# A decoder step's mixing stage: u projections by feature block, and the state-space part ranked ahead of banded attention

## The chip, the cores and the metric

The kernel runs on one core of a Trainium2 chip. A core has five engines with instruction queues of their own, each worked off strictly in order: TensorE (PE in the profile; PEld is its weight load) for matrix products, VectorE (DVE), ScalarE (ACT), GpSimd (POOL) and SyncE (SP, which here only issues DMAs). The metric is the time of one execution on the device in microseconds; several runs of each kernel are compared by their medians.

## The reference

One step of a one-layer hybrid decoder for 1024 prompt tokens and 32 sample tokens (8 sequences of 4), 1056 in all, 1024 features wide, in 32-bit floats:

```python
h = h + 0.5 * rms_norm(swiglu(rms_norm(h, ffn1_pre_g), ...), ffn1_post_g)
z = rms_norm(h, mix_pre_g) @ w_in                # 512 u, 512 q, 128 k, 128 v
y, s_re, s_im = s5_scan(u, s0_re, s0_im, ...)    # 32 groups of 16 features, 64 complex states each
g = gelu(y)
y_ssm = g * sigmoid(g @ ssm_w_glu + ssm_b_glu)
o = swa_prompt(q, k, v, sinks)                   # window 128, 8 heads on 2 key heads, sinks
mixed = concatenate([rms_norm(y_ssm), rms_norm(o)]) @ w_out
h = h + rms_norm(mixed, mix_post_g)
h = h + rms_norm(memory_attend(...), xa_post_g)  # 4 heads into 256 memory tokens
h = h + 0.5 * rms_norm(swiglu(rms_norm(h, ffn2_pre_g), ...), ffn2_post_g)
```

The sample tokens go through the same layer with a cached window and a state of their own. The memory keys and values of the prompt are projected in the same launch and are outputs too.

## The kernel before

Activations lie transposed, features on the 128 partitions and tokens along the free axis, in three token groups of 352, which are taken in the order 2, 0, 1 (`ORDER`). A large product is computed three times with operands split into a rounded high part and a remainder (`mm3`, line 105): high by high, high by low, low by high. Each weight is loaded by SP, split by ScalarE (line 99) and VectorE (line 100).

The program runs: first feed-forward, then the **mixing stage**, then the output projection w_out, cross-attention and the second feed-forward. In the mixing stage stand, in the order of the text:

1. the q, k and v projections, with the rotary part (`rope`, lines 807 to 831);
2. attention over 128-query blocks, of which 5, 6 and 7 come first. Each block is worked in two *halves* of four heads. A half has its scores (line 877, two products of 128 x 512 into PSUM tiles called ac), their masked maximum on VectorE (line 880), exponentials on ScalarE (line 850), sums and reciprocal (848 to 854), scaling on VectorE (856), eight transposes on TensorE (893), two copies out (897, one on VectorE, one on ScalarE), the value products into the tile po (900), and two copies into qT (903). `attend` issues the scores of the next half ahead of the combination of the present one; there are two score buffers, which lie in the block K3, and two ac tiles;
3. the u projections: four blocks of 128 features by three token groups, twelve products of 24 matmuls each into two PSUM tiles px, with an eviction that scales by the norm (line 922). Their inputs are the split activations X of the three token groups;
4. the state-space part `ssm()`: for each of four feature blocks a `gather` (transposes, lines 947 to 965, through PSUM tiles su and buffers ut, us, ug of the pool s1), then for pairs of groups `advance` (978 to 988: two products into sab, a rotation, a scan along the blocks, a rotation back) and `emit` (1000 to 1015), then `spread` (1022, 1028, 1031), and the gelu;
5. the memory projections `memory_kv` (lines 105 and 495, into px, with evictions 485 and 499): 384 matmuls of 256 columns that depend on nothing in this stage;
6. the sample tokens' attention, then blocks 0 to 2, a norm (`arm`, lines 151, 125 to 133, 143), blocks 3 and 4, a norm;
7. the gated linear unit, GLU (1162 to 1180), whose split inputs go into K2, K3 and a new X.

Pool s1 is allocated on the left side once pool x1, which holds the X of this stage, has been released; a tile of s1 waits for the readers of the tiles that lay in its place. The keys of attention (kz) lie in K2, the u of the four blocks in K0 and K1.

The order on each engine isn't that of the text. A scheduler gives each instruction the running number `tc.cur_priority` as its rank, walks through a model of the engines in time, and lets each engine take the lowest rank that is ready. The call `at(base + P)` sets the running number, so the constants `P_...` rank the parts of this stage against each other: attention 0, state space 10000, u 20000, GLU 25000, memory projections 30000. Attention of step 6 goes on where step 2 left off (`at(mark)`), right behind it.

Of the kernel before, what the change touches and what calls it, by code (L numbers as in the profile page):

```python
# [17 lines left out]
NH = 22  # L18
EPS = 1e-6
ORDER = (2, 0, 1)  # L20
P_ATT, P_SSM, P_U, P_GLU, P_MEM = 0, 10000, 20000, 25000, 30000
MAGIC = 12582912.0
PASSES = ((0, 0), (0, 1), (1, 0))
G_FFN1_PRE, G_FFN1_POST, G_MIX_PRE, G_MIX_POST, G_XA_PRE, G_XA_POST, G_FFN2_PRE, G_FFN2_POST, G_MEM, G_CAT = range(10)
# [3 lines left out]
def decoder_step(tc, a, o):  # L28
# [42 lines left out]
    def pbank():  # L71
        return pbase.tile([128, 512], F32, name="px", tag="px", bufs=2)
# [22 lines left out]
    def loadw(src, raw=None, width=1024):  # L95
        if raw is None:
            raw = stage(src, width=width)
        w = wp.tile([128, 2, 1024], F32R, name="w", tag="w", bufs=6)[:, :, :width]
        sc.activation(w[:, 0], raw, AF.Copy)  # L99
        v.tensor_sub(w[:, 1], raw, w[:, 0].bitcast(F32))  # L100
        return w
# [651 lines left out]
    for i in range(2):  # L753
        c = slice(512 * i, 512 * i + 512)
# [38 lines left out]
    def proj(w, t, p=None):  # L793
        p = bank() if p is None else p
        for k in range(8):
            mm3(p[:, :NT], w, k * 128, mid[t], k, k == 0, k == 7)
        return p[:, :NT]
# [119 lines left out]

    at(base + P_U)
    wu = [loadw(a["w_in"][c]) for c in range(4)]
    for t in ORDER:  # L920
        for c in range(4):
            v.tensor_mul(uT[c // 2][:, c % 2, t * NT:(t + 1) * NT], proj(wu[c], t, pbank()), mid[t][2])
    xp[0].release()
    sp_ = xp[0] = pool("s1", "left")
# [602 lines left out]
```

## Time and profile before

| | |
|---|---|
| median of 3 runs | 2352.02 us (2351.97 to 2355.77) |
| the profiled execution | 2350.7 us, span 2348.9 us |
| first feed-forward, to the q, k, v projections | up to about 815 us of the span |
| q, k, v projections | about 815 to 895 |
| u projections | 895 to 946 |
| state space, attention, memory projections | 946 to 1152 |
| GLU, then w_out | 1152 to 1181, from 1181 |

A row of a timeline has the start in us, the length in us, the engine, the line, the operation, output and inputs by the program's names without their numbers, the shape, and how many instructions were merged; in brackets the idle time ahead of it and what ended it. A row of a group has the count, the busy time in us, the mean length of one in ns, and idle time before with its releaser. A 32-bit matmul of plain operands leaves two records; one on split operands, or a transpose, leaves one. Records on an engine overlap, so a group's lengths add up to more than the time it takes. The granted clock is TensorE's, as a share of full speed.

### The profile page before, as it was taken

How to read it: one execution, taken by the hardware profiler on the slowest of the kernel's cores; microseconds unless marked ns; L12 is line 12 of the kernel's file. 1: busy time of each engine (PE TensorE's matmuls, PEld its weight loads, DVE VectorE, ACT ScalarE, POOL GpSimd, SP SyncE). 2: the span in 40 equal slices, each digit the busy share in tenths (PEclk: the TensorE clock that was granted, in tenths of full speed). 3: DMA queues.
4: the chain of work that ended last, by engine and by line, in shares of the span. 5: the costliest groups of instructions: out<-in, count | busy, mean ns of one | idle time of the engine just before them, and what ended most of it. 6: DMA issues, size and time to landing. Idle time of an engine off the chain costs nothing.

```text
span 2348.9 us, 37434 instructions
## 1 busy us (share of the span) xinstructions
PE 2281.9 (97%) x14425; PEld 2178.3 (93%) x14425; DVE 1631.5 (69%) x4004; ACT 839.4 (36%) x1645; POOL 15.9 (1%) x54
## 2 busy tenths in 40 slices
PE   8999999999999899999799989999999899999997
PEld 8999999999999899888699869999999899999996
DVE  8756556665664877777768855588866987776464
ACT  6322111211212433535545323354433434344443
POOL 0000000000000000000000000000000000000000
PEclk9999999999999999999899999999999999999998
DMA  4222212221213321544135562165544243326663
GB/s 171 70 71 68 62 57 71 82 76 59 73 55 93 112 87 58 193 147 127 35 97 167 183 221 72 55 213 169 175 132 144 85 143 106 115 97 200 185 193 119
DMA packets 112194, 272.39 MB, mean 116 GB/s; under 512 B 13168, under 2 KB 54128, under 8 KB 110576
## 3 DMA queue, kind: packets, MB, share of 16 engines
q1 hardware_dynamic: 78976, 227.81, 30.8%
q10 hardware_dynamic: 33040, 42.20, 5.1%
q8 instruction: 113, 1.85, 0.3%
q14 instruction: 65, 0.53, 0.1%
HBM read 229.87 MB, written 43.20 MB: 116 GB/s over the span
## 4 chain that ended last, share of the span: by engine, by line
PE 85%; DVE 7%; DMA 5%; ACT 2%; issue 1%; ACTq 0%; SPq 0%; DVEq 0%
PE mm L105 39%; PE mm L241 14%; PE mm L330 13%; PE mm L385 3%; PE px L105 3%; DMA raw<-wd 2%; DVE w L100 1%; PE cv L1279 1%; PE cs L1254 1%; PE px L1176 1%; DVE K L219 1%; PE ac L877 1%; PE px L495 1%; PE px L385 1%; DMA K<-h 1%
## 5 line engine op out<-in xcount | busy, mean ns | idle before, releaser
L105 PE MATMUL mm<-X,w 128*128 128x352 f32 x6384 | 1060.8, 325 | 12.3 <-ACT X L195 6.5
L105 PEld LDWEIGHTS mm<-X,w 128*128 128x128 f32 x6384 | 1028.3, 189 | 30.2 <-ACT X L195 8.5
L99 ACT ACTIVATE w<-raw 128x1024 fp32r<-128x1024 f32 (+1 forms) x271 | 266.2, 988 | 500.4 <-PE mm L105 212.2
L100 DVE TENSOR_TENSOR w<-raw,w 128x1024 fp32r<-128x1024 f32 (+1 forms) x271 | 307.1, 1136 | 136.2 <-ACT w L99 134.0
L241 PE MATMUL mm<-hid,w 128*128 128x352 f32 x2112 | 358.6, 328 | 12.6 <-DVE K L247 6.2
L241 PEld LDWEIGHTS mm<-hid,w 128*128 128x128 f32 x2112 | 345.6, 189 | 19.7 <-DVE K L247 8.8
L330 PE MATMUL mm<-xq,w 128*128 128x352 f32 x1584 | 263.5, 323 | 0.0
L330 PEld LDWEIGHTS mm<-xq,w 128*128 128x128 f32 x1584 | 255.9, 188 | 0.4 <-ACT w L310 0.4
L247 DVE TENSOR_TENSOR K<-K,mm 128x352 f32<-128x352 f32 x320 | 158.3, 518 | 52.2 <-PE mm L241 51.3
L514 DVE TENSOR_TENSOR K<-K 128x128 f32<-128x128 f32 (+7 forms) x796 | 171.6, 250 | 11.3 <-DMA sp<-K 2.0
L385 PE MATMUL mm<-xq,w 128*128 128x352 f32 x924 | 159.1, 326 | 4.6 <-ACT w L99 3.4
L385 PEld LDWEIGHTS mm<-xq,w 128*128 128x128 f32 x924 | 148.8, 188 | 10.7 <-ACT w L99 5.9
L310 ACT ACTIVATE w<-raw 128x512 fp32r<-128x512 f32 x154 | 90.0, 625 | 119.1 <-PE mm L330 83.1
L231 DVE TENSOR_TENSOR q<-mm,rs 128x352 f32<-128x352 f32 x88 | 46.0, 522 | 117.6 <-PE mm L105 117.6
L311 DVE TENSOR_TENSOR w<-raw,w 128x512 fp32r<-128x512 f32 x154 | 101.1, 686 | 6.2 <-ACT w L310 3.9
L116 DVE TENSOR_TENSOR tot<-tot,sq 128x352 f32<-128x352 f32 x179 | 93.0, 520 | 10.4 <-ACT sq L114 7.0
L114 ACT ACTIVATE sq<-K 128x352 f32<-128x352 f32 x170 | 81.9, 490 | 42.7 <-DVE tot L116 34.7
L229 DVE TENSOR_TENSOR sg<-mm,rs 128x352 f32<-128x352 f32 x88 | 46.0, 523 | 72.9 <-PE mm L105 72.5
L183 ACT ACTIVATE hid<-sg 128x352 fp32r<-128x352 f32 x88 | 43.6, 496 | 145.7 <-DVE sg L232 115.7
L230 ACT ACTIVATE sg<-sg 128x352 f32<-128x352 f32 x88 | 43.2, 492 | 138.9 <-DVE sg L229 120.4
L195 ACT ACTIVATE X<-K,c_gains 128x352 fp32r<-128x352 f32 x80 | 44.0, 580 | 45.4 <-DVE K L220 42.8
L184 DVE TENSOR_TENSOR hid<-sg,hid 128x352 fp32r<-128x352 f32 x88 | 45.8, 521 | 15.6 <-ACT hid L183 15.4
(326 smaller groups left out, 2179.1 us busy)
## 6 DMA issues: line engine op xcount, KB each, us to landing
raw<-wd SPq DMA_DIRECT2D x66, 512.0 KB
raw<-wu SPq DMA_DIRECT2D x65, 512.0 KB
raw<-wg SPq DMA_DIRECT2D x64, 512.0 KB
sp<-sp SPq DMA_DIRECT2D x16, 848.0 KB
h<-K ACTq DMA_DIRECT2D x9, 1408.0 KB
raw<-hs SPq DMA_DIRECT2D x66, 176.0 KB
raw<-wd SPq DMA_DIRECT2D x44, 256.0 KB
K<-xT SPq DMA_DIRECT2D x24, 352.0 KB
```

What stands on the lines that cost most here:

```text
L99: sc.activation(w[:, 0], raw, AF.Copy)
L100: v.tensor_sub(w[:, 1], raw, w[:, 0].bitcast(F32))
L105: pe.matmul(p, w[:, wa, col:col + 128], x[xa][:, k, :n], start=first and i == 0, stop=last and i == 2)
L114: sc.activation(q, c, AF.Square)
L116: eng.tensor_add(tot, tot, q)
L241: pe.matmul(p[c][:, :NT], w[j][:, wa, c * 128:c * 128 + 128], h[:, j, xa], start=j == 0 and i == 0, stop=j == 1 and i == 2)
L247: v.tensor_add(acc[:, c], acc[:, c], p[c][:, :NT])
L310: sc.activation(w[:, 0], x, AF.Copy)
L311: v.tensor_sub(w[:, 1], x, w[:, 0].bitcast(F32))
L330: pe.matmul(p, w[a_][:, wa, k * 128:k * 128 + 128], x[b_][xa][:, k], start=start and k == 0 and i == 0, stop=stop and k == 3 and i == 2, s ...
L385: pe.matmul(p[c][:, :NT], w[:, wa, c * 128:c * 128 + 128], (hi, lo)[xa], start=k == 0 and q == 0, stop=k == NH - 1 and q == 2)
L514: v.tensor_tensor(out, x, y, op)
```

## The change

Two edits. The ranks become u 0, state space 5000, attention 10000; GLU and memory projections keep theirs. And the twelve u projections are written with the feature block in the outer loop and the token group in the inner, where it was the other way round. No instruction is added or taken away.

```diff
-P_ATT, P_SSM, P_U, P_GLU, P_MEM = 0, 10000, 20000, 25000, 30000
+P_U, P_SSM, P_ATT, P_GLU, P_MEM = 0, 5000, 10000, 25000, 30000
...
     at(base + P_U)
     wu = [loadw(a["w_in"][c]) for c in range(4)]
-    for t in ORDER:
-        for c in range(4):
+    for c in range(4):
+        for t in ORDER:
             v.tensor_mul(uT[c // 2][:, c % 2, t * NT:(t + 1) * NT], proj(wu[c], t, pbank()), mid[t][2])
     xp[0].release()
     sp_ = xp[0] = pool("s1", "left")
```

## The prediction

> **What bounds the kernel now.** I read the page first, then the busy times by stage, then TensorE and VectorE in the stage that the change touches.
>
> ```profile
> span 2348.9 us, 37434 instructions
> PE 2281.9 (97%) x14425; PEld 2178.3 (93%) x14425; DVE 1631.5 (69%) x4004; ACT 839.4 (36%) x1645; POOL 15.9 (1%) x54
> ```
>
> TensorE is busy for 97% of the span. A mere reordering adds and removes no instruction, so it can win only TensorE's idle time or lose by adding some. The stages around the change (columns: stretch, length, busy time of each engine with its records, clock, DMA share, GB/s):
>
> ```profile
> 895.00:946.17 51.17, 51.17 (x312) 49.10 (x311) 48.04 (x130) 19.53 (x51) 0.00 (x0) 1.00 0.26 83
> 946.17:1117.42 171.25, 170.98 (x1343) 139.47 (x1342) 132.29 (x500) 80.90 (x223) 3.60 (x12) 1.00 0.46 154
> 1117.42:1151.46 34.04, 25.41 (x140) 16.70 (x138) 28.87 (x85) 22.82 (x61) 0.00 (x0) 0.88 0.20 59
> 1151.46:1181.44 29.98, 26.81 (x151) 26.81 (x151) 18.08 (x58) 15.19 (x30) 0.00 (x0) 0.80 0.04 8
> ```
>
> The first row is the u projections, the second the state-space part, attention and the memory projections together: TensorE is full in both. The third is the **tail of attention**: the memory projections, the only work that can fill every gap, are used up, and TensorE is idle for 8.6 us of 34.0 while VectorE is at 85%. The fourth is the gated unit (GLU). The tail's two ends, on TensorE, and VectorE's last steps in it:
>
> ```profile
> 1116.50 1.07 PE L495 MATMUL px<-w 128*128 128x256 f32 x7
> 1117.42 1.02 PE L877 MATMUL ac<-K,qT 128*128 128x512 f32 x2
> 1118.27 0.60 PE L893 MATMUL ac<-c_ident,K 128*128 128x128 f32 x4
> 1149.49 1.97 PE L900 MATMUL po<-K,vT 128*64 128x256 f32 x8 [2.04 <-DVE K L897]
> 1154.63 3.89 PE L1176 MATMUL px<-K,w 128*128 128x352 f32 x12 [3.17 <-ACT sq L1179]
> 1122.23 0.48 DVE L499 TENSOR_SCALAR mo<-px,rc 128x256 f32<-128x256 f32 x1
> 1145.31 1.14 DVE L856 TENSOR_SCALAR K<-K,ta 128x256 f32<-128x256 f32 x4
> 1148.65 0.68 DVE L897 COPY K<-ac 128x512 f32<-128x512 f32 x1
> ```
>
> From the last half block's value product (1149.49) the order of work is the same in both programs, so the question is when that product ends (1151.46 now).
>
> **The change part by part.** *u projections by feature block.* The twelve products stay, 288 matmuls. With the three token groups of block 0 done first, the state-space gather could begin after three of twelve products. The order on TensorE (px: a projection, su: a gather's transposes), before and now:
>
> ```order
> L105 MATMUL px_9606<-X1_8393,w_9359 128x352
> L947 MATMUL su_9697<-c_ident_94,K0_8467 128x128 x4
> ...
> L105 MATMUL px_9658<-X1_8393,w_9369 128x352
> L151 MATMUL px_10632<-ones_96,tot_10588 128x1
> ...
> L947 MATMUL su_9703<-c_ident_94,K0_8467 128x128 x4
> ```
>
> ```order
> L105 MATMUL px_9476<-X0_8082,w_9359 128x352
> L947 MATMUL su_9697<-c_ident_94,K0_8467 128x128 x4
> ...
> L105 MATMUL px_9658<-X1_8393,w_9369 128x352
> L877 MATMUL ac_9118<-K2_8466,qT_8465 128x512
> L151 MATMUL px_10632<-ones_96,tot_10588 128x1 x2
> L947 MATMUL su_9703<-c_ident_94,K0_8467 128x128 x4
> ```
>
> The first four transposes move up by seven products, but the second four still come behind the last one: their predecessor's copy goes into pool s1, which lies where the projections' inputs X lay, and all X are now in use to the end. The first state-space matmul (L978) moves up by 8 of TensorE's instructions. TensorE is full here, so I take 0 for this part; a late eviction would cost at most one product, 51.17 / 12 = 4.3 us, and a gain is excluded by 51.17 busy of 51.17.
>
> *State space before attention.* This pushes attention's halves back, past the memory projections. The end of those (L495) on TensorE, before and now (po: a half's value product, sy: a state-space emission):
>
> ```order
> L495 MATMUL px_11114<-w_11146,w_10586 128x256
> L877 MATMUL ac_11623<-K2_8466,qT_8465 128x512
> L893 MATMUL ac_11644<-c_ident_94,K3_9053 128x128 x4
> L1000 MATMUL sy_10533<-ug_10289,sp_10494 128x8
> ...
> L900 MATMUL po_11643<-K1_8468,vT_8460 64x256 x2
> ```
>
> ```order
> L495 MATMUL px_11114<-w_11146,w_10586 128x256
> L900 MATMUL po_11434<-K1_8468,vT_8460 64x256 x2
> L877 MATMUL ac_11454<-K2_8466,qT_8465 128x512
> L1000 MATMUL sy_10515<-ug_10289,sp_10455 128x8
> ...
> L900 MATMUL po_11434<-K3_9053,vT_8460 64x256 x2
> L877 MATMUL ac_11458<-K2_8466,qT_8465 128x512
> ```
>
> po_11643 is half 0 of block 3, with three halves behind it: four halves in the tail. po_11434 is half 0 of block 1: eight halves (one nearly done), and two emissions in place of one. So much leaves the full stage and goes behind it, by TensorE's groups in 946.17 to 1117.42:
>
> ```profile
> L877 PE MATMUL ac<-K,qT 128*128 128x512 f32 (+1 forms) x47 | 24.0, 590 | 0.2 <-DVE ta L880 0.2
> L893 PE MATMUL ac<-c_ident,K 128*128 128x128 f32 x88 | 14.4, 278 | 0.0
> L900 PE MATMUL po<-K,vT 128*64 128x256 f32 x88 | 13.7, 401 | 0.0
> 1105.47 0.28 PE L1000 MATMUL sy<-ug,sp 128*128 128x8 f32 x2
> 1108.01 1.67 PE L495 MATMUL px<-w 128*128 128x256 f32 x12
> 1112.58 0.93 PE L143 MATMUL ac<-c_ident,ti 118*128 118x118 f32 x6
> ```
>
> Seven score matmuls (two records each) at 24.0/47 = 0.51 a record: 7.1 us. 24 transposes at 0.164: 3.9. 16 value matmuls (32 records) at 0.156: 5.0. One emission, 1105.47 to 1108.01: 2.5. One reduction pair for a norm: 0.93 and about as much, 1.8. Together 20.3; but records overlap. The score at 1117.42 lasts 1.02 and the transposes behind it start after 0.85, at 1118.27, a factor of 0.83, which gives 16.9. I take **17 us**: the memory projections end at 1117.4 - 17 = 1100.4. The bounds are 20.3 (no overlap) and 171.25/1343 x 106 records = 13.5.
>
> *The longer tail.* VectorE's groups in the old tail, and one reduction with its successor's start:
>
> ```profile
> L184 DVE TENSOR_TENSOR X<-q,X 128x352 fp32r<-128x352 f32 x8 | 3.7, 517 | 0.0
> L100 DVE TENSOR_TENSOR w<-raw,w 128x1024 fp32r<-128x1024 f32 x3 | 3.7, 1221 | 0.0
> L856 DVE TENSOR_SCALAR K<-K,ta 128x256 f32<-128x256 f32 x12 | 3.4, 347 | 0.0
> L897 DVE COPY K<-ac 128x512 f32<-128x512 f32 x4 | 2.7, 682 | 0.0
> L1153 DVE SCALAR_TENSOR_TENSOR q<-qT,c_gains,rs 128x352 f32<-128x352 f32 x5 | 2.7, 572 | 0.0
> L1031 DVE SCALAR_TENSOR_TENSOR K<-K,c_gains,su 128x512 f32<-128x512 f32 x2 | 2.3, 1142 | 0.0
> L1168 DVE TENSOR_TENSOR X<-K,X 128x352 fp32r<-128x352 f32 x4 | 1.8, 516 | 0.0
> 1123.60 0.48 DVE L880 CUSTOM_DVE_ANT_0 K<-ac,c_mask,c_sinks 128x256 f32<-128x256 f32 x1 [0.74 <-PE ac L877]
> 1124.01 0.08 DVE L880 DVE_READ_ACCUMULATOR2_ANT ta<- 128x1 f32 x1
> ```
>
> A row overlaps the next by some 0.075 us (0.48 long, successor after 0.41), so each costs its mean less that, and the accumulator's read nothing. From the eviction of the last memory product (L499) to the copy of the last half (L897) VectorE now has 24 reductions (9.8), 4 weight splits L100 (4.6), 24 scalings (6.4), 7 copies (4.2), 2 L1031 (2.1), 12 L184 (5.3), 4 L1167 and 4 L1168 (2.8), 5 L1153 (2.5), 3 L116 (1.3) and small ones (4.7): **43.7 us**. By the same count the old program has 23.2, and took 1122.23 to 1148.65, 26.4.
>
> The waits in the new tail, walked along the two orders: 4.4 at its head, where TensorE has two emissions, four scores, eight transposes and three value pairs (5.1 + 3.8 + 1.2 + 1.9 = 12.0) before VectorE, with 8.7 of its own, can reduce the fourth score, and a weight split (1.1) stands ahead of that; 1.7 where the halves of blocks 0 to 2 drain and the norm of token group 0 runs before block 3's first reduction; 5.8 over the last four halves. With the 2.8 from the last copy to the end of its product (1148.65 to 1151.46) the tail is 43.7 + 11.9 + 2.8 = 58.4, near **58**. It replaces 34.0: **58 - 34 - 17 = +7 us**. The bounds: with no waits 46.5, so -4.5 (-8 with 20.3 for 17); at the old tail's 34.04/4 = 8.5 a half for 7.5 halves 64, so +13 (+16.5 with 13.5).
>
> What works the other way is within the sum. The preparation of the GLU's operands, which now stands between the last half's scaling and copy, has moved ahead. VectorE's last rows, before and now:
>
> ```order
> L856 TENSOR_SCALAR K3_9053<-K3_9053,ta_11716 128x256 x4
> L184 TENSOR_TENSOR X2_11913<-q_11926,X2_11912 128x352
> ...
> L1153 SCALAR_TENSOR_TENSOR q_12041<-qT_8465,c_gains_79,rs_11588 128x352
> L897 COPY K1_8468<-ac_11751 128x512
> L184 TENSOR_TENSOR X0_12028<-q_12037,X0_12027 128x352
> ```
>
> ```order
> L184 TENSOR_TENSOR K2_11815<-K1_8468,K2_11815 128x352 x2
> L897 COPY K1_8468<-ac_11732 128x512
> L853 TENSOR_TENSOR ta_11716<-ta_11716,ta_11717 128x4
> L854 RECIPROCAL ta_11716<-ta_11716 128x4
> L856 TENSOR_SCALAR K3_9053<-K3_9053,ta_11716 128x256 x4
> L897 COPY K1_8468<-ac_11751 128x512
> ```
>
> But the GLU cannot start for it: its first operand is written into K2, which holds the keys until the last score, so it stays behind attention.
>
> *The clock.* In the old tail the granted clock was 0.88 and behind it 0.80; inside the tail it fell early, by these rows:
>
> ```profile
> 1133.66 0.44 PE L893 MATMUL ac<-c_ident,K 128*128 128x128 f32 x2 [1.06 <-DVE K L856]
> 1135.39 0.59 PE L1176 MATMUL px<-K,w 128*128 128x352 f32 x2 [1.29 <-ACT K L183]
> 1135.00:1140.00 5.00, 4.61 (x21) 4.59 (x22) 4.63 (x12) 4.97 (x15) 0.00 (x0) 0.66 0.02 3
> ```
>
> With 0.88 for the 17 us of matmuls that move into the tail they would take 17/0.88 - 17 = 2.3 us more, most of it beside VectorE; I add nothing and keep 2 for the range. The Trainium skill (TensorE: Matmul & The Clock Gate, "Why this matters for your kernels") has gaps above some 3 us between bursts drop the clock; by that rule alone the added tail, with gaps of one or two, would stay at full clock and cost exactly the sum. The trace differs here: 0.66 stands behind gaps of 1.06 and 1.29 us that followed each other closely.
>
> The profiled execution is span 2348.9, time 2350.7; the median of the runs shown, 2352.0, is 1.3 more. 2350.7 + 7 + 1.3 = **2359**.
>
> **The rivals.** *VectorE packs the tail* (faster): the moved work is ready in plenty, attention's halves overlap, and VectorE has no waits; it decides if the tail ends under 51 us. -4.5 gives 2347.5. For it: VectorE idled only 5.2 of 34.0 us. Against: the drain before block 3, and the 4.4 us at the head, where TensorE is the slower one.
>
> *The change does little* (no change): the new priorities hardly act, since both parts wait on their own chains: the last state-space emission moves up by only 22 of TensorE's instructions. Then fewer than 17 us leave the full stage and the tail grows by little more than that, 0 to +3, some 2353.5. Against: the four halves more behind the last L495 stand in the order.
>
> *Each half at the old tail's pace* (slower still): 8.5 us a half because exponentials, copies and transposes follow one another with two score buffers, and the clock falls in the gaps: +13, 2365. Against: the old four halves carried 14 us of GLU preparation, most of which is not doubled.
>
> **How the numbers follow.** Forecast (+3 to +10) 0.47, each half at the old pace (above +10) 0.14, little change (-4.7 to +3) 0.27, packed (below -4.7) 0.12. What a measurement can tell from no change is 0.2%, 4.7 us, so 2347.3 to 2356.7 is the same. Of the forecast's band about four fifths lie above +4.7, 0.37: slower 0.37 + 0.14 = 0.51, same 0.37, faster 0.12. The range goes from the packed tail, 2347, to somewhat beyond the old pace, 2368.
>
> **What would show it.** In the changed profile the last L495 row should end near 1100, and the last value product of eight records near 1158; between them TensorE busy about 40 us, VectorE about 44 to 47; the u projections should end at 946 as now, and from the last value product to the first w_out product 30 us as now. I am wrong if the last L495 ends after 1106 (then the middle has stalls of its own), or if the tail is under 51 us.

## The result: slower by 0.62%, about twice the forecast

| | before | changed |
|---|---|---|
| median | 2353.89 us (2351.97 to 2356.68, 4 runs) | 2366.45 us (2365.32 to 2367.93, 4 runs) |
| profiled execution, span | 2350.7, 2348.9 us | 2366.9, 2365.1 us |
| ratio | | 1.0062 (95%: 1.0047 to 1.0077) |

The ratio is estimated from all the runs; the two medians alone are 12.6 us or 0.53% apart, which its interval holds. The sign was forecast, the size was not: +7 us were forecast, +12.6 came. 2366.45 lies inside the range (2347 to 2368), close to its upper end and to the rival "each half at the old tail's pace" (2365).

### The profile page after: what moved, and what is told of

Same layout as the page of the kernel before. It is cut to its first block, busy times and chain, and to the rows that moved or that the text cites. A ratio compares the mean times of both kernels' runs of the same rounds, so it can differ in the third digit from the quotient of the medians.

```text
span 2365.1 us, 37428 instructions
## 1 busy us (share of the span) xinstructions
PE 2290.9 (97%) x14425; PEld 2184.0 (92%) x14425; DVE 1632.9 (69%) x4004; ACT 839.3 (35%) x1645; POOL 15.9 (1%) x54
## 4 chain that ended last, share of the span: by engine, by line
PE 87%; DVE 6%; DMA 4%; ACT 2%; issue 1%; SPq 0%; ACTq 0%; DVEq 0%
PE mm L105 41%; PE mm L241 14%; PE mm L330 12%; PE mm L385 3%; PE px L105 3%; DMA raw<-wd 2%; PE ac L877 1%; PE cs L1254 1%; PE cv L1279 1%; DVE w L100 1%; PE px L385 1%; PE px L495 1%; DVE K L219 1%; PE px L1176 1%; ACT w L99 1%
## 5 line engine op out<-in xcount | busy, mean ns | idle before, releaser
L514 DVE TENSOR_TENSOR K<-K 128x128 f32<-128x128 f32 (+7 forms) x796 | 171.7, 250 | 10.9 <-DMA sp<-K 1.6
L184 DVE TENSOR_TENSOR hid<-sg,hid 128x352 fp32r<-128x352 f32 x88 | 45.9, 521 | 14.8 <-ACT hid L183 14.6
```

Of the source, the lines that this page charges most:

```text
L514: v.tensor_tensor(out, x, y, op)
```

## The profile of the changed kernel

The busy times by stage (columns as in the prediction). The cuts are the ends of the u projections, of the last memory product (L495), of the last half's value product (L900), and of the GLU:

```profile
895.00:946.17 51.17, 51.17 (x312) 49.19 (x311) 47.10 (x126) 18.49 (x43) 1.71 (x8) 1.00 0.40 132
946.17:1100.50 154.33, 153.00 (x1239) 130.16 (x1237) 116.87 (x430) 68.80 (x183) 1.92 (x6) 1.00 0.44 152
1100.50:1165.50 65.00, 50.33 (x244) 28.73 (x240) 47.04 (x160) 36.16 (x110) 0.00 (x0) 0.82 0.13 37
1165.50:1195.40 29.90, 26.92 (x151) 26.93 (x152) 18.61 (x57) 14.96 (x30) 0.00 (x0) 0.83 0.04 9
```

The u projections are untouched. The full stage is 17 us shorter (171.25 to 154.33), the tail 31 us longer (34.04 to 65.00), the GLU as long as before. From the first w_out product to the end it is 2365.1 - 1195.3 = 1169.8, where it was 2348.9 - 1181.4 = 1167.5. So -17 + 31 + 0 + 2 = 16 us between the two profiled executions; the medians are 12.6 apart, since the profiled run of before was 3 us under its median. A part of the last 2 us stands at the start of w_out: the changed kernel's TensorE waits 1.66 us at 1200.8, for VectorE's L184, and 0.55 at 1201.9, where that of before waits only 0.55, at 1186.3.

TensorE in the middle of the new tail, from the last memory product on (rows between them left out; last column: idle time ahead and what ended it):

```profile
1098.38 1.91 PE L495 MATMUL px<-w 128*128 128x256 f32 x14
...
1122.72 0.93 PE L900 MATMUL po<-K,vT 128*64 128x256 f32 x4 [1.80 <-ACT X L183]
1123.95 1.12 PE L900 MATMUL po<-K,vT 128*64 128x256 f32 x4 [0.31 <-ACT K L897]
1127.32 1.32 PE L151 MATMUL ac<-ones,tot 128*118 128x1 f32 x6 [2.25 <-DVE tot L116]
1128.51 2.06 PE L877 MATMUL ac<-K,qT 128*128 128x512 f32 x2
1131.65 2.04 PE L877 MATMUL ac<-K,qT 128*128 128x512 f32 x2 [1.08 <-DVE ti L133]
1133.49 1.47 PE L143 MATMUL ac<-c_ident,ti 118*128 118x118 f32 x6
1134.78 2.87 PE L877 MATMUL ac<-K,qT 128*128 128x512 f32 x4
1141.47 1.97 PE L893 MATMUL ac<-c_ident,K 128*128 128x128 f32 x8 [3.83 <-DVE K L856]
...
1164.22 1.08 PE L900 MATMUL po<-K,vT 128*64 128x256 f32 x8 [0.76 <-ACT K L897]
```

A score pair here is the two records that one score product leaves; block 3 has four of them, two a half. Two things show. The norm of token group 0 (L151, its reciprocal root on VectorE, then L143) writes into ac, one of the two PSUM banks through which all scores and transposes go. It stands in the queue ahead of block 3's scores, and from 1127.3 to its eviction at 1135.4 it holds one bank: the first two score pairs of block 3 (1128.5, 1131.7) go one at a time through the other. And a score pair takes 2.06 us, where it took 1.02 to 1.13 elsewhere: the clock is at one half. The same stretch, in slices of 5 us:

```profile
1120.00:1125.00 5.00, 2.89 (x16) 1.19 (x15) 4.81 (x13) 3.90 (x11) 0.00 (x0) 0.80 0.00 1
1125.00:1130.00 5.00, 2.75 (x10) 1.70 (x8) 3.62 (x13) 2.88 (x6) 0.00 (x0) 0.50 0.01 3
1130.00:1135.00 5.00, 3.92 (x10) 2.28 (x10) 2.53 (x14) 0.13 (x1) 0.00 (x0) 0.50 0.00 0
1135.00:1140.00 5.00, 2.64 (x4) 0.73 (x4) 4.18 (x17) 3.55 (x13) 0.00 (x0) 0.84 0.00 0
1140.00:1145.00 5.00, 2.85 (x9) 1.93 (x10) 4.01 (x15) 3.15 (x11) 0.00 (x0) 0.50 0.01 3
1145.00:1150.00 5.00, 5.00 (x13) 1.60 (x12) 1.58 (x7) 0.45 (x2) 0.00 (x0) 0.50 0.00 0
```

From 1125 to 1135 neither VectorE (6.2 of 10 us) nor ScalarE (3.0) nor TensorE (6.7) is full: all wait on one another. So two suspects, the shared bank and the clock, and the experiments had to part them; and first the two edits of the change.

## The experiments

Each was timed against runs of the kernel before on the same chip, whose medians were 2352.1 to 2354.1 us. So a difference of 2 us or less between two experiments is not clear of their baselines.

### 1. Which edit: the loop alone, the ranks alone, u first alone

The loop alone keeps the old ranks, the ranks alone keep the old loop. The third:

```diff
-P_ATT, P_SSM, P_U, P_GLU, P_MEM = 0, 10000, 20000, 25000, 30000
+P_U, P_ATT, P_SSM, P_GLU, P_MEM = 0, 5000, 10000, 25000, 30000
```

> The loop order alone (feature block outer), with the old ranks. My theory (the whole loss comes from ranking attention behind the state-space part): no change, 0 +- 2 us against the kernel before, u projections ending at 946 us, four halves of attention behind the last memory product and a tail of 30 to 34 us. Rival (the loop order takes part in the loss, because the gather's late transposes and evictions then collide with the last projections): +4 us or more, seen as TensorE idle between 895 and 960 us.

> The five ranks alone, with the old loop order. My theory: the whole loss of the change, +10 to +14 us against the kernel before; last memory product near 1100 us, eight halves behind it, tail about 65 us with the granted clock at one half for over 20 us of it. Rival (loop order and ranks share the loss): +4 to +8 us.

> Only the u projections get the first rank; attention stays ahead of the state-space part, old loop order. My theory (what counts is attention against state space): 0 +- 2 us against the kernel before, four halves in the tail. Rival (the u projections ahead of the first scores delay attention by up to 51 us of TensorE work, and that is what lengthens the tail): +4 us or more, five or more halves behind the last memory product.

Measured: loop alone 2356.4 us, ratio 1.0014 (1.0005 to 1.0022); ranks alone 2371.8, 1.0076 (1.0061 to 1.0090); u first 2352.6, 0.9993 (0.9984 to 1.0003). So the loss is the exchange of attention and state space, as I thought; giving u the first rank does not change the time. But the loop order is not nothing. With the old ranks it costs 3.6 us, which is outside both expectations (no change, or 4 us and more with TensorE idle between 895 and 960: it isn't). With the new ranks it gives 5.3 back (2371.8 to 2366.45); there the two intervals overlap, but the same sign comes again with the norm's bank moved (section 3, 2363.2 to 2359.7). My figure for the ranks alone (+10 to +14) was too low: +19. The tails and the last memory product, by the rows of the two (the cuts are those of the table above):

```profile
1122.28:1158.40 36.12, 23.97 (x109) 14.78 (x106) 27.54 (x77) 24.25 (x59) 0.00 (x0) 0.77 0.21 67
```

```profile
1104.94:1168.09 63.15, 46.56 (x220) 26.04 (x220) 44.86 (x152) 33.88 (x104) 0.00 (x0) 0.84 0.11 32
```

In the first (loop alone) the last memory product ends at 1122.3, 4.7 us after that of before: by its order, the last state-space emission and a score now stand ahead of it. The tail holds less TensorE work (24.0 us against 25.4), and yet is 2 us longer. In the second (ranks alone) the last memory product ends at 1104.9, 4.6 after the changed kernel's, with one emission in the tail where the changed kernel has two; the tail is 1.9 shorter. Both pairs would fit one reading, that an emission in the tail lies beside VectorE's work and costs less than ahead of the last memory product. It is not shown: in the first pair the tail grew although an emission left it, and in "u first" (two emissions in the tail, four halves as before) the last memory product came 5.1 us earlier, at 1112.5, and the tail was 8.2 longer, 42.3.

Of the 6.3 us between the profiled executions of the ranks alone and of the changed kernel, 1.8 stand ahead of the first w_out product and 4.5 behind it (1174.3 us from there to the end against 1169.8). This holds for the whole study: from the first w_out product to the end the profiled executions take from 1167.5 us (before, u first) to 1176.1 (the ranks with the norm's bank moved), and no run explains it. So a few us between two kernels are not the tail's alone.

### 2. The clock: a held product, and idle products

A memory product was held back to fill TensorE where the clock fell:

```diff
+            if f == 3:
+                late = [loadw(a["w_mem_v"][f, h]) for h in range(2)]
+                yield
+                one = late[0][0:1, 0, 0:1]
+                v.scalar_tensor_tensor(one, qT[0:1, 1, 256:257], 0.0, one.bitcast(F32), op0=ALU.mult, op1=ALU.add)
...
-    memory_kv(L)
+    kv = memory_kv(L)
+    next(kv)
...
     arm(0)
+    here = tc.cur_priority
+    at(base + P_MEM + 4000)
+    assert next(kv, 0) == 0
+    at(here)
```

> The changed kernel, but the last of the four memory value projections (48 matmuls, some 6.5 us of TensorE work, its weights split as early as before) waits until the first half of block 2 is combined: one element of its weights is rewritten with its own value plus zero times an element of that half's output. So it fills TensorE in the drain between block 2 and block 3, where the clock fell. Theory A (the loss beyond my forecast is the clock, halved after gaps of 1.2 to 2.3 us): the clock stays at 1.0 until 1136 us at least, a score pair takes 1.1 us and not 2.07 there, the tail is 60 us or less from the last early memory product although it carries 6.5 us more, and the whole is 9 to 14 us under the changed kernel (2353 to 2358). Theory B (the halves' own chain sets the tail and the clock only accompanies it): the tail stays 63 to 66 us, only the 6.5 us taken from the full stage are won, 2359 to 2361. Theory C (the held product gets in attention's way): the tail grows by about as much, 2364 to 2368.

Measured: 2373.0 us, 1.0093 (1.0078 to 1.0107), 6.5 slower than the changed kernel: worse than all three. TensorE's rows from the held product on, and one of ScalarE's (L500; the scores are L882 here, and L132 is a VectorE step of the norm's root):

```profile
1126.49 3.37 PE L500 MATMUL px<-w 128*128 128x256 f32 x26
1130.75 0.75 PE L151 MATMUL ac<-ones,tot 128*118 128x1 f32 x6 [0.90 <-DVE tot L116]
1131.36 1.10 PE L882 MATMUL ac<-K,qT 128*128 128x512 f32 x2
1135.53 2.04 PE L882 MATMUL ac<-K,qT 128*128 128x512 f32 x2 [3.06 <-DVE ta L885]
...
1145.25 2.04 PE L882 MATMUL ac<-K,qT 128*128 128x512 f32 x2 [4.48 <-DVE ti L132]
```

```profile
1133.38 1.06 ACT L99 ACTIVATE w<-raw 128x1024 fp32r<-128x1024 f32 x1 [2.54 <-DMA raw<-w_out]
```

The held product did fill TensorE, and the clock was back at 1.0 from 1125 to 1132. But it also held four of the six weight buffers, which the first w_out weights need. These now were loaded and split from 1127 to 1141, in the middle of the norm and of block 3's first half, on VectorE and ScalarE, and TensorE waited up to 4.5 us for the norm's root. There is a second wait ahead of the held product, which the changed kernel does not have: TensorE stood still for 4.74 us (1115.6 to 1120.4), where ScalarE took an activation of the GLU and two table loads of 1.28 us each ahead of the last exponential of a half. The run doesn't say how the 6.5 us divide between the two, and says nothing on the price of the clock; it shows that a filler's own resources can come due at the worst place.

Then idle products that hold no such buffer: eight of 24 matmuls on the GLU's weights into px, at the lowest rank.

```diff
+        y = tuple(wgl[1][:, i].rearrange("p (k n) -> p k n", n=256) for i in range(2))
+        for c in range(8):
+            p = pbank()
+            for k in range(8):
+                mm3(p[:, :256], wgl[0], k * 128, y, k % 4, k == 0, k == 7, 256)
```

> The changed kernel plus eight idle products at the lowest rank behind the memory projections: 24 matmuls each on the first GLU weights, into a memory-projection bank, read by nobody; some 26 us of TensorE work that exists only to keep TensorE busy in the tail, above all between block 2 and block 3 (84 of the 192 matmuls stand there). They use no weight buffer that others wait for, unlike the held product. Clock theory (the halved clock costs some 7 us of the changed kernel's tail of 65): the granted clock stays at 1.0 to 1140 us, a score pair there takes 1.1 us instead of 2.07, and in spite of the added work the tail is 62 us or less, the time 2360 to 2364. Chain theory (waits for VectorE, ScalarE and the two score banks set the tail; the clock costs little): tail 65 to 70 us, 2366 to 2372, although the clock is at 1.0.

Measured: 2380.5 us, 1.0115 (1.0101 to 1.0131). Too much: TensorE was busy for all of 1100 to 1140, so it became the limit itself. The time rose by 14 us for 26 us of added work, which lies outside both expectations and which both theories could explain. Inconclusive; so a smaller dose, 28 products of 128 x 128 (56 records), gated by block 2:

```diff
     arm(0)
+    here = tc.cur_priority
+    at(base + P_MEM + 4000)
+    p = pbank()
+    for k in range(28):
+        pe.matmul(p[:, k % 4 * 128:k % 4 * 128 + 128], ident, qT[:, 0 + k % 2, 256:384], start=True, stop=True)
+    at(here)
```

> The changed kernel plus 28 idle 128x128 products on block 2's finished outputs, into a memory-projection bank, read by nobody, lowest rank: 18 stand where TensorE waits ahead of block 2's last value product (1120.8 to 1122.7 us), 10 behind it, where it waits 2.3 us for the norm. About 5 us of work where TensorE idles 4, without the 26 us that made TensorE itself the limit in the earlier filling. Clock theory (the halved clock from 1122 us on is the larger part of the 8.4 us by which the bank shortened the tail): the clock stays at 1.0 until 1130 us, the three score pairs take 1.1 us, the tail is 59 to 62 us, 2360 to 2363. Bank theory (the clock's part is under 3 us, and the added work costs about as much): tail 64 to 67 us, 2365 to 2369.

Measured: 2364.1 us, 1.0053 (1.0041 to 1.0066), between the two expectations and 2.4 under the changed kernel, with intervals that overlap (against the runs of before beside each it is 12.0 and 12.6). TensorE there:

```profile
1121.71 4.29 PE L1132 MATMUL px<-qT,c_ident 128*128 128x128 f32 x36 [0.45 <-ACT qT L903]
1125.92 1.08 PE L900 MATMUL po<-K,vT 128*64 128x256 f32 x8
1126.94 2.50 PE L1132 MATMUL px<-qT,c_ident 128*128 128x128 f32 x20
1129.46 0.75 PE L151 MATMUL ac<-ones,tot 128*118 128x1 f32 x6
1130.07 1.10 PE L877 MATMUL ac<-K,qT 128*128 128x512 f32 x2
1132.26 1.10 PE L877 MATMUL ac<-K,qT 128*128 128x512 f32 x2 [1.08 <-DVE ti L129]
1133.19 0.82 PE L143 MATMUL ac<-c_ident,ti 118*128 118x118 f32 x6
1134.44 1.95 PE L877 MATMUL ac<-K,qT 128*128 128x512 f32 x4 [0.42 <-DVE ta L880]
1140.93 1.98 PE L893 MATMUL ac<-c_ident,K 128*128 128x128 f32 x8 [4.54 <-DVE K L856]
```

Here the clock stayed at 1.0 until 1140 and each score pair takes 1.10 us, so the cure of the clock is complete in this stretch. From the norm's first product to block 3's first transposes it is 1129.46 to 1140.93, 11.5 us, against 1127.32 to 1141.47, 14.2, at half clock. The clock's price is thus 2.7 us here. Most of it was paid back at once: the idle products put the norm off by 2.1 us, so that the transposes come only 0.5 us earlier. The scores still go one by one, and by section 3 that is the larger part.

### 3. The bank

```diff
     def arm(t):
         arms[t] = rstd(sqsum([qT[:, c, t * NT:(t + 1) * NT] for c in range(4)]), factor=2.0, tag="rs", bufs=3,
-                       p=wbank("ac", 2))
+                       p=pbank() if t == 0 else wbank("ac", 2))
```

> The changed kernel, but the norm of token group 0 (between blocks 2 and 3) takes its bank from the memory projections' pair, free by then, and not one of the two banks that scores and transposes share. Bank theory (from 1127 to 1135 us one of the two banks is held by that norm, and three of block 3's four first scores go one by one through the other): block 3's scores are issued before the norm's sum, the tail is 57 to 61 us, the time 2358 to 2362. Clock theory alone: the bank makes no difference, 2365 to 2368, tail 64 to 66 us.

> The ranks alone with the old loop order, and the norm's bank from the memory projections' pair. If the bank is the reason why eight halves cost more than my count of 58 us, it gives as much here as with the new loop order, 6 to 9 us of the 18 by which the ranks alone were slower: 2362 to 2366. If the loop order was part of that mechanism: less than 4 us, 2368 to 2372.

Measured: on the changed kernel 2359.7 us, 1.0028 (1.0017 to 1.0039), so 6.8 less. On the ranks alone 2363.2, 1.0046 (1.0032 to 1.0060), 8.6 less. (Against the runs of before beside each it is 6.2 and 8.0.) Both times are inside what the bank theory said. TensorE and the tail of the first:

```profile
1123.46 2.07 PE L877 MATMUL ac<-K,qT 128*128 128x512 f32 x2
1125.46 0.89 PE L900 MATMUL po<-K,vT 128*64 128x256 f32 x4
1126.28 1.98 PE L877 MATMUL ac<-K,qT 128*128 128x512 f32 x4
1128.92 1.10 PE L877 MATMUL ac<-K,qT 128*128 128x512 f32 x2 [0.66 <-DVE ta L880]
1129.86 0.68 PE L151 MATMUL px<-ones,tot 128*118 128x1 f32 x6
1132.88 2.05 PE L893 MATMUL ac<-c_ident,K 128*128 128x128 f32 x8 [2.34 <-DVE K L856]
```

```profile
1100.03:1156.94 56.91, 46.73 (x244) 27.32 (x244) 45.94 (x160) 36.63 (x110) 0.00 (x0) 0.91 0.13 43
```

All four score pairs of block 3 are out before the norm, which no longer stands ahead of them, and the first transposes come at 1132.9 and not at 1141.5, 8.6 us earlier. The tail is 56.9 us, VectorE busy 45.9 and idle 11.0. The clock fell here too (the pair at 1123.46 takes 2.07 us), so the gain doesn't come from the clock alone. Bank and order changed together: no run on the changed kernel moves the scores ahead of the norm and leaves it the shared bank. And a part of the gain is lost again behind the tail: the first w_out product comes 10.9 us earlier than in the changed kernel (1184.4 against 1195.3), the end of the execution 7.0.

### 4. No drain, and a faster kernel

Between blocks 2 and 3 the last half of block 2 is worked to its end before block 3's first scores are issued, which I call the drain. It was taken out as well:

```diff
-    attend((0, 1, 2))
-    arm(0)
-    attend((3, 4))
+    early = attend((0, 1, 2), last=False)
+    next_ = scores(3, 0)
+    combine(*early)
+    arm(0)
+    early = scores(3, 1)
+    combine(*next_)
+    attend((4,), early)
```

(`attend` takes the half still held, and hands it back when it is not the last call.) On the changed kernel, with the bank:

> The changed kernel with that bank and, further, no drain between blocks 2 and 3: the first scores of block 3 are issued before the last half of block 2 is combined, and the norm of token group 0 comes behind them. Theory (the stretch from 1122 to 1142 us, one drained pipeline with a norm in it, is where the tail exceeds my 58 us): tail 50 to 56 us, the time 2351 to 2357, and the granted clock at 1.0 for most of it. Rival (a half costs 8 to 8.5 us wherever it stands, by VectorE's steps and the exponentials): tail 62 to 65 us, 2363 to 2367.

Measured: 2360.3 us, 1.0032 (1.0018 to 1.0046): between the two expectations, and no different from the bank alone. The tail was 56.3 us. With the bank free, taking the drain out gains nothing that can be told from noise there.

On the kernel before, with the old ranks and the old loop order, each edit alone and both:

> The kernel before with only the norm of token group 0 in the other bank. Its order still has four halves behind the last memory product, and two emissions in place of one. If the count of halves behind the last memory product sets the time: 2351 to 2356, tail 34 to 37 us. If the bank by itself is the lever (as it is in the changed kernel, where it was worth 7 us): 2343 to 2348.

> The kernel before with only the drain between blocks 2 and 3 taken out; the norm keeps its old bank. Four halves and one emission behind the last memory product, as before. By the count of halves: 2350 to 2355, tail 32 to 36 us. If the drain by itself is the lever: 2343 to 2348.

> The kernel before (old ranks, old loop order) with the same two edits, bank and no drain. By its order only two halves, not four, stand behind the last memory product. Theory (every half that leaves the tail is filled by memory products, and a half in the tail costs 8.5 us of time but only some 5 us of TensorE work): the last memory product ends near 1126 us, the tail is 18 to 22 us, the time 2344 to 2349. Rival (the norm's bank is taken from the memory projections while these still run, and their products wait for it): TensorE idle of 3 us or more before the last memory product, 2351 to 2355.

Measured: bank alone 2352.6 us, 0.9993 (0.9985 to 1.0002); no drain alone 2354.8, 1.0001 (0.9993 to 1.0010); both 2342.0, 0.9954 (0.9940 to 0.9968). Either alone is nothing, and leaves the tail at 34 us with four halves in it (32 records of L900 behind the last memory product); with both together 20 records are left there, two halves and a part of a third. The time is 2 us below what the theory gave (2344 to 2349). The stages of the kernel with both:

```profile
946.20:1122.86 176.66, 176.45 (x1356) 140.70 (x1354) 136.97 (x516) 85.11 (x244) 2.73 (x9) 1.00 0.44 149
1122.86:1142.46 19.60, 17.11 (x104) 12.56 (x102) 17.17 (x52) 13.94 (x34) 0.00 (x0) 0.83 0.30 102
```

The full stage is 5 us longer and still full, the tail 14 shorter, its last value product 9.0 us earlier than before. TensorE does not wait for the norm's bank (0.2 us idle in 176.7). This is the fastest kernel of the study, 11.4 us under the kernel before beside it. Whether the other orders add to it:

> Both edits with the u projections ranked first and attention ahead of the state-space part (old loop order). Three halves and two emissions behind the last memory product in its order. By the count of halves, at 8.5 us a half of which some 5 are TensorE work that then is missing from the full stage: 3 to 4 us over the kernel with both edits and the old ranks, 2344 to 2347. Rival (ranking the u projections first is worth about 1 us by itself, as it was with the old edits): 2340 to 2343.

> Both edits with the loop by feature block and the old ranks. Two halves and one emission behind the last memory product, as in the kernel with both edits alone. By the count of halves: the same, 2340 to 2344. Rival (the loop order costs 3 us by itself, as it did alone): 2344 to 2348.

Measured: with u first 2346.0, 0.9967 (0.9956 to 0.9978), 4 us behind, which is the time that the count of halves gave. But that is luck: 28 records of L900 stand behind the last memory product, eight more than in the kernel with both edits, and yet the tail is 20.5 us and its last value product comes 3.1 us earlier (1139.4). The loss stands behind it, 34.0 us to the first w_out product instead of 27.7, and from that to the end 1175.7 instead of 1170.3. With the loop by feature block 2347.1, 0.9963 (0.9951 to 0.9975): 5 us behind, against the count of halves and in the range of its rival. Its last value product too comes 3.1 us earlier (1139.4), but from there to the first w_out product it takes 32.5 us, and from that to the end 1173.4. Both intervals overlap that of the kernel with both edits. So the number of halves behind the last memory product does not rank these three kernels, and what does is open.

## Why the prediction was right in sign and wrong in size

- **The memory projections end at 1100.4, 17 us earlier.** Right: the last row is 1098.38 + 1.91 = 1100.3. The count of instructions and the overlap factor carried this. The count was taken from the order of both edits together, and so held the second emission in the tail, which by experiment 1 comes from the loop order.
- **The loop order is worth 0.** Wrong: 3.6 us are lost by it with the old ranks, and some 5 won with the new. I looked only for idle time of TensorE in the u projections, where there is none (51.17 of 51.17 again). The step that failed is "a late eviction would cost at most one product ... a gain is excluded". The orders differ 170 us later, in which emission falls on which side of the last memory product; that this is the cause is not shown.
- **The tail grows to 58.** It grew to 65.0, and this is where the size was missed. VectorE in the changed kernel, from the last memory product to the reduction of the fourth score behind it (the head), on to block 3's first reduction, and on to the last copy (columns as before); and two of its rows:

```profile
1100.30:1113.63 13.33, 12.66 (x82) 8.02 (x84) 10.19 (x31) 8.66 (x23) 0.00 (x0) 1.00 0.43 129
1113.63:1130.61 16.98, 10.78 (x56) 5.85 (x52) 14.98 (x49) 11.27 (x30) 0.00 (x0) 0.77 0.15 41
1130.61:1163.39 32.78, 25.94 (x100) 14.41 (x100) 20.82 (x81) 15.48 (x56) 0.00 (x0) 0.75 0.00 0
1133.73 0.48 DVE L880 CUSTOM_DVE_ANT_0 K<-ac,c_mask,c_sinks 128x256 f32<-128x256 f32 x1 [2.16 <-PE ac L877]
1150.15 0.48 DVE L880 CUSTOM_DVE_ANT_0 K<-ac,c_mask,c_sinks 128x256 f32<-128x256 f32 x1 [3.02 <-PE ac L877]
```

  By the prediction's own terms: VectorE's work 43.7, measured 44.6 (the sum of the three rows less 1.4 ahead of the eviction L499, which the count leaves out); the head 4.4, measured 4.5 (13.33 - 10.19 and that 1.4); the drain and the norm before block 3's first reduction 1.7, measured 2.0; **"5.8 over the last four halves", measured 12.0**; from the last copy to the end of its product 2.8, measured 1.9. The term that failed is the 5.8, the wait of VectorE over the halves of blocks 3 and 4. I had walked their order and given the norm its latency, but no bank: block 3's first scores go one at a time (2.16 us of waiting at 1133.7), and a score at half clock is waited for too (3.02 at 1150.2). With the norm in another bank the same stretch, from block 3's first reduction to the last copy, has these sums:

```profile
1125.77:1155.02 29.25, 24.11 (x110) 14.03 (x106) 23.09 (x94) 18.99 (x62) 0.00 (x0) 0.88 0.00 1
```

  VectorE waits 6.2 us there, near the 5.8 (4.5 again at the head, and 0.4 before block 3's first reduction, behind which the norm now lies), and the tail is 56.9, 1.5 under the forecast's 58.4. So the count of VectorE's work and the other waits were sound, and the missing 6.6 us of the tail went with this one bank. That the time with it, 2359.7, is also the forecast (2359) within a us is partly luck: its first w_out product comes 4 us earlier than forecast (1184.4 against 1100.4 + 58 + 30), and some 6 us more than before stand behind it (1173.7 against 1167.5), which the forecast did not have.
- **The clock: "I add nothing and keep 2 for the range".** It was 0.82 in the tail, at one half for most of 1122.5 to 1150, and TensorE was busy 50.3 us there where about 40 were forecast. It lay on the path: 2.7 us in the stretch that was cured of it. I take these 2.7 as a part of the bank's 6.8, since with the bank free the clock fell for less time (0.91 over the tail, TensorE busy 46.7); no run separates that sum further, and none cures the stretch from 1141 to 1150, where TensorE is busy without a break at half clock from 1145 on.
- **From the last value product to w_out 30 us as now.** Right, 1165.3 to 1195.3. I had not looked behind it, where some 2 us were lost.
- **The rivals.** "Each half at the old tail's pace", 2365, came nearest, but not for its reason: not exponentials, copies and transposes at two score buffers, but one norm in the shared banks, beside the fallen clock that it named too. "Packed" and "little change" are out; the range held by 1.5 us.
- **My own first explanation** after the result, that the halved clock was the larger part of the miss, fell with the smaller dose of idle products.

## What to carry to other kernels

When work is pushed behind the last filler, walk not only its instructions but every buffer and bank that they share, in the new order: a slow side chain (here a norm, 8 us from its first product to its eviction) that was harmless under filler holds one of two banks on the path. Look at how much dependent work stands behind the last filler, but don't take its count for the time: it gave the gain of the two edits together, and did not hold in the traces of two orders that were tried on top of them. Two edits that do nothing alone can be worth 11 us together. A gain read in one stage can be lost again behind it, so follow it to the end. Before holding filler back, ask which buffers it keeps and who is next in line for them.

## What the runs showed of the hardware that I had not expected

The clock fell to one half at 1122.5 us behind gaps of TensorE of 1.23, 0.52 and 1.80 us within 8 us, none of them long. Two rows of TensorE in the changed kernel (the third gap is in the row at 1122.72 above), and two slices of 2.5 us:

```profile
1115.88 0.65 PE L1028 MATMUL su<-c_ident,yt 128*128 128x128 f32 x4 [1.23 <-DVE K L1031]
1118.12 0.41 PE L1047 MATMUL su<-K,c_ident 128*128 128x32 f32 x2 [0.52 <-DVE K L1031]
```

```profile
1120.00:1122.50 2.50, 0.92 (x8) 0.67 (x7) 2.31 (x8) 2.50 (x8) 0.00 (x0) 1.00 0.01 1
1122.50:1125.00 2.50, 1.97 (x8) 0.52 (x8) 2.50 (x7) 1.40 (x4) 0.00 (x0) 0.59 0.00 0
```

With some 7 us of idle products laid into this stretch it stayed at 1.0 there, and fell in the next gap, of 4.54 us (1136.4 to 1140.9; 0.53 from 1140 to 1145). That fits little work of TensorE over some 3 us (0.92 of 2.5, and this in transposes alone) better than one long gap, but no run varies the one against the other. The Trainium skill (TensorE: Matmul & The Clock Gate, "A second HAM failure mode: psum-queue depth-cycling") tells of frequent micro-idles that make the clock go down and up. This trace agrees, with 0.80, 0.50, 0.50, 0.84 and 0.50 in the slices from 1120 to 1145; by the rule of single gaps above 3 us, which the prediction weighed, the fall at 1122.5 would not have come.
